# Weights of the second output projection moved into the spent tiles of keys and queries, and split during the attention

## Chip, cores, metric

The kernel runs on one core of a Trainium2 chip. The metric is device microseconds of one execution, median over runs; lower is better.

## What is computed

Two layers of a diffusion backbone on 512 latent and 256 context tokens of width 1024, all in 32-bit floats. What matters here, of each layer:

```python
y  = concatenate([y_fn, y_na, y_gla]) @ w_out      # Fourier mixing, neighbourhood attention (6 heads x 64), linear attention
x  = x + g_m * y
x  = x + g_f * swiglu(ada_modulate(x, norm_ffn, sh_f, sc_f), ffn_w1, ffn_w3, ffn_w2)
if need_ctx:                                       # first layer only
    yc = concatenate([fourier_mix(fc), ctx_attn(qch, kch, vch), yc_gla]) @ w_out
    cx = cx + cg_m * yc
    cx = cx + cg_f * swiglu(ada_modulate(cx, ...), ffn_w1, ffn_w3, ffn_w2)
```

## The kernel before

**Arithmetic.** Every 32-bit operand of a product is split into a high part (a copy on ACT, L195) and a low part (source minus high part, on DVE, L189; on POOL where the caller says so). `split` at L197 does both, and a product is then three matmuls (`mm3`, L181). Tiles are feature-major: 128 features by 512 latent columns (or two halves of 256) or 256 context columns.

**The second output projection.** `w_out` is applied in two pieces. The first (`woa`, 5 blocks of 128 rows, generator `wo`) covers Fourier mixing and linear attention; its products are dropped between the units of the attention by `fill`. The second (`wob`, 3 blocks of 128 rows, generator `wb`) covers the neighbourhood attention and runs behind it. `wout` (L969) makes both. For each of 8 output tiles m it has a raw weight (128 x 384, 192 KB), its split, and one product with each stream n, each ending in a residual update on DVE (L192, `u<-m,u,u` and the like). In layer 0 the streams are context (256 columns) and latents (512 columns); in layer 1 only latents, in two halves.

**Buffers of `wb` before.** In layer 0 (`whole` false) two raw tiles and two split tiles `whl` rotate; raw tile m + 2 is loaded when weight m + 1 is split, in the loop over products. `split_at` = 6 gives context and latent tile in turn for m = 0 to 5, then context tiles 6 and 7, then latent tiles 6 and 7. In layer 1 (`whole` true) all eight weights are split into eight tiles `whlw` during the attention, out of the two raw tiles in turn.

**The attention.** It has 3 pairs of heads with 5 blocks each in layer 0 (15 units), 4 in layer 1 (12 units). Unit n on PE: scores of unit n (`a<-st,st`), transposes of unit n - 1 (`b<-u,p`, L1244), some products of `wo` (`m<-u,whl`), then values of unit n - 1 (`y<-pT,vn`). DVE adds the bias and takes the maximum (`s<-a,bias`, L1212), ACT takes the exponential (`p<-s,nm`), DVE scales it (`p<-p,rcl`, L1223), and the transposed tile `pT` is copied out of PSUM by ACT or DVE in turn. `kn` and `qn` (6 tiles of 128 x 512 each, pool `nap`) hold normalised keys and queries; pairs 1 and 2 are transposed out of them by `features_of_heads` (L942) during the units of the pair before, and stored by 8 DMAs `st<-kt` and then `st<-qt` on SP (L909). After the last of these `kn` and `qn` are read no more, though they stay allocated to the end of the attention.

**What stands behind `wb`.** The sum of squares of each updated tile (`nsq` on ACT; added up on DVE for context, as `nacc` on POOL for latents in layer 0), the norm factors (`nms`, `nrs`, `ndg`), the modulation of eight context and eight latent tiles (`nt<-u,u,a` DVE, `u<-nt,u` ACT, `u<-nt,u,u` DVE), and the first two steps of the FFN. Those use four weights of 128 x 1024 (`W_first`, L1368, two steps of two), loaded by DMA `raw<-in_w` into three raw tiles (L430); ACT makes the high parts, POOL the low parts.

**What sets the order.** PE's order in the attention and in `wb` is the order of the code (`tc.manual_schedule`, L1291 and L1328). Elsewhere a scheduler at build time orders each engine's instructions by its own model of time and by priorities; `W_first` has the priority of the start of `wb` (`early_w`, L1336). At run time each engine, and SP with its DMAs, goes through its list in order.

Of the kernel before, what the change touches and what calls it, by code (L numbers as in the profile page):

```python
# [16 lines left out]
F32 = mybir.dt.float32  # L17
F32R = mybir.dt.float32r
# [7 lines left out]
KD = 8  # L26
# [116 lines left out]
def hybrid_kernel(tc, d, out, dbg=None):  # L143
    nc = tc.nc
# [283 lines left out]
    def wraw(p, src, n, rb, cap):  # L428
        r = mk(p, [128, cap], F32, "raw", rb)[:, :n]
        nc.sync.dma_start(out=r, in_=src)  # L430
        return r
# [23 lines left out]
    for l in range(DEPTH):  # L455
# [508 lines left out]

        gm = lambda s, k: modT[l][:, s, 16 + k:17 + k]

        loaded = []

        def wout(src, nk, streams, kinds, whole=False, split_at=KD, begin=0):  # L969

            nb, cap = (KD, 128 * nk) if whole else (2, 640)
            tag = "whl" + "w" * whole
            raw = lambda m: wraw(wop, src[m], 128 * nk, 2, cap)
            part = lambda r: wsplit(wop, r, (nk, 128), nb, cap, tag)
            if whole:
                w = [part(raw(m)) for m in range(KD)]  # L980
            else:
                raws = [raw(m) for m in range(2)]
                w = [part(raws[0])]
            early = {}
            for m in range(0, begin, 2):
                yield None, 0
                bank = (PM, PB, PM)[m // 2]()
                for i in range(2):
                    ps = bank[:, 256 * i:256 * i + 256]
                    for j in range(nk - 1):  # L990
                        mm3(ps, w[m + i][0][:, j], w[m + i][1][:, j], streams[0][0][j][:, 0], streams[0][0][j][:, 1],
                            i == j == 0, False)
                    early[m + i, 0] = ps, nk - 1
            yield None, 0

            def product(m, n, ys, xs, s):
                wh, wl = w[m]
                ps, j0 = early.pop((m, n), (None, 0))
                ps = dense(kinds)[:, :xs(m).shape[-1]] if ps is None else ps
                for j in range(j0, nk):  # L1000
                    mm3(ps, wh[:, j], wl[:, j], ys[j][:, 0], ys[j][:, 1], j == 0, j == nk - 1)
                    if j < nk - 1:
                        yield None, ps.shape[-1]
                stt(xs(m), ps, gm(s, m), xs(m), ALU.mult, ALU.add)

            todo = [(m, n) for m in range(split_at) for n in range(len(streams))]
            todo += [(m, n) for n in range(len(streams)) for m in range(split_at, KD)]
            if begin:
                todo[:2 * begin:2], todo[1:2 * begin:2] = todo[:begin], todo[begin:2 * begin]
            for m, n in todo:  # L1010
                if m == KD - 1:
                    loaded.append(src)
                if m + 1 == len(w) < KD:
                    w.append(part(raws[m + 1]))
                    if m + 2 < KD:
                        raws.append(raw(m + 2))
                yield from product(m, n, *streams[n])
                yield (m, n), streams[n][1](m).shape[-1]

# [134 lines left out]

        nst = ExitStack()
        np_ = pool(nst, f"na{l}", "left")

        credit = [0.0]

# [123 lines left out]

        half = lambda ts, h: [t[..., 256 * h:256 * h + 256] for t in ts]
        streams = both_x(ync, ynl) if ctx_q else [(half(ynl, h), lambda m, h=h: xl[m][:, 256 * h:256 * h + 256], 0) for h in range(2)]
        wb = wout(d["wob"][l], 3, streams, "mbmya", not ctx_q, 6 if ctx_q else 0, 0 if ctx_q else 4)

        nb = 5 if ctx_q else 4
        units = [(pr, b) for pr in range(3) for b in range(nb)]
# [1 line left out]
        with tc.manual_schedule(engines={mybir.EngineType.PE}):  # L1291
            for n in range(len(units) + 1):
                if n < len(units):
                    pr, b = units[n]
                    pairs[pr].scores(b)
                if n:
                    pq, c = units[n - 1]
                    pairs[pq].transposed(c)
                if n == len(units) and not ctx_q:
                    for _ in wo:  # L1300
                        pass
                if loaded and not ahead:
                    ahead.append(next(wb))
                if n == len(units) and not ctx_q:
                    next(wb)
                if n < len(units) and b == 0 and pr < 2:
                    pairs[pr + 1] = Heads(pr + 1)
                fill(2.4 if ctx_q else 2.3)
                if pr < 2 and n < len(units):
                    for _ in range((1, 1, 1, 1, 0)[b]):  # L1310
                        next(pairs[pr + 1].prepare, None)
                if n == nb - 1:
                    with tc.issue_after(last_stack[0]):
                        load_streams(range(3, KD))
                if n:
                    pairs[pq].values(c)
            for _ in wo:
                pass
            if not ctx_q:
                for _ in range(1):  # L1320
                    next(wb)
# [164 lines left out]
```

## Time and profile before

| | |
|---|---|
| median of 3 runs | 1663.78 us (1663.53 to 1668.41) |
| the profiled execution | 1662.66 us |
| its span | 1660.6 us |
| PE busy | 97% |
| DVE, ACT, POOL busy | 55%, 35%, 14% |

The span runs from the first to the last instruction that the profiler saw; 2.06 us of the profiled execution lie outside. Layer 0's attention lies at 312 to 397 us of the span and its `wb` at 397 to 429; layer 1's attention lies at 1200 to 1275. A PE busy for 97% of the span means that a change can only remove the remaining gaps, the stretches at half clock, or work. In a list of one engine's rows, the bracket at a row's end is how long the engine was idle before it and what ended that.

### The profile page before, as it was taken

To read this page: it belongs to the slowest core of one execution; us is meant where nothing else is said; L and a number is where in the kernel's file an instruction comes from. 1 tells how busy PE (TensorE), PEld (TensorE's weight loads), DVE (VectorE), ACT (ScalarE), POOL (GpSimd) and SP (SyncE) were. 2 spreads that over 40 slices of the span, in tenths; PEclk is the share of its full clock that TensorE was granted. 3 is DMA by queue.
4 is the path that set the end of the run, shared out by engine and by line. 5 is a ranking of instruction groups with operands and counts; after the bars stand their busy time and mean duration, and the time that the engine had idled before them with its cause. 6 is when DMAs were issued, how large, how long until landed. Compare 5 with 4: busy or idle time off the path is not lost.

```text
span 1660.6 us, 25071 instructions
## 1 busy us (share of the span) xinstructions
PE 1613.8 (97%) x9938; PEld 1402.3 (84%) x9938; DVE 920.6 (55%) x1665; ACT 583.9 (35%) x1048; POOL 232.2 (14%) x275
## 2 busy tenths in 40 slices
PE   6999999999999999999999999999999999999999
PEld 5878889787888888888888889899787988888887
DVE  5699974776774664355333434464577743434432
ACT  5365223544542411211122324842445522222220
POOL 0143431003240400000000011333102000000000
PEclk9999999999999999999999999999999999999999
DMA  9445544653152454144221411222663233233321
GB/s 329 159 151 164 164 155 124 192 134 112 52 175 76 153 188 143 62 148 146 65 75 45 127 53 40 70 97 94 194 182 119 84 113 99 91 93 98 102 89 51
DMA packets 79904, 199.66 MB, mean 120 GB/s; under 512 B 10344, under 2 KB 21164, under 8 KB 78764
## 3 DMA queue, kind: packets, MB, share of 16 engines
q1 hardware_dynamic: 79788, 198.07, 37.9%
q8 instruction: 78, 1.28, 0.3%
q14 instruction: 38, 0.31, 0.1%
HBM read 174.84 MB, written 14.29 MB: 114 GB/s over the span
## 4 chain that ended last, share of the span: by engine, by line
PE 81%; DVE 7%; DMA 6%; ACT 2%; issue 2%; SPq 1%; POOL 0%; DVEq 0%; ACTq 0%; POOLq 0%
PE a L181 26%; PE m L181 23%; PE b L181 19%; PE y L181 11%; DVE adac L192 2%; DMA adaw<-in_adaw 2%; DVE u L192 1%; DVE whl L189 1%; PE b L1244 1%; DMA raw<-in_wg 1%; DMA raw<-in_wob 1%; DMA raw<-in_w 1%; ACT whl L195 1%; DMA qn<-scr_q 1%; DVE u L189 1%
## 5 line engine op out<-in xcount | busy, mean ns | idle before, releaser
L195 ACT ACTIVATE whl<-raw 128x1024 fp32r<-128x1024 f32 (+7 forms) x222 | 205.0, 928 | 392.2 <-PE a L181 132.3
L189 DVE TENSOR_TENSOR whl<-raw,whl 128x1024 fp32r<-128x1024 f32 (+7 forms) x201 | 225.2, 1122 | 91.7 <-ACT whl L195 91.5
L181 PE MATMUL m<-u,whl 128*128 128x512 f32 (+1 forms) x1278 | 264.1, 359 | 1.9 <-DVE whl L189 1.9
L181 PE MATMUL a<-u,whl 128*128 128x512 f32 (+1 forms) x1299 | 246.6, 346 | 2.4 <-ACT u L195 1.5
L181 PEld LDWEIGHTS m<-u,whl 128*128 128x128 f32 x1278 | 211.9, 191 | 35.3 <-DVE whl L189 2.2
L181 PEld LDWEIGHTS a<-u,whl 128*128 128x128 f32 x1299 | 208.6, 189 | 32.6 <-ACT u L195 1.7
L181 PE MATMUL b<-u,whl 128*128 128x512 f32 (+1 forms) x915 | 181.8, 349 | 1.8 <-ACT whl L195 0.9
L192 DVE SCALAR_TENSOR_TENSOR adac<-adaw,u,adac 128x512 f32<-128x512 f32 x196 | 159.0, 828 | 42.1 <-DMA adaw<-in_adaw 41.0
L181 PEld LDWEIGHTS b<-u,whl 128*128 128x128 f32 x915 | 150.1, 189 | 25.2 <-ACT whl L195 1.1
L181 PE MATMUL b<-whl,u 128*128 128x384 f32 (+1 forms) x696 | 144.9, 345 | 1.3 <-DVE u L192 0.9
L181 PE MATMUL m<-whl,u 128*128 128x384 f32 (+2 forms) x672 | 138.0, 344 | 2.8 <-ACT u L195 2.5
L181 PEld LDWEIGHTS b<-whl,u 128*128 128x128 f32 x696 | 122.2, 189 | 8.7 <-issue 4.7
L181 PEld LDWEIGHTS m<-whl,u 128*128 128x128 f32 x672 | 116.5, 189 | 15.3 <-issue 9.8
L181 PE MATMUL a<-g,whl 128*128 128x512 f32 (+1 forms) x594 | 126.9, 370 | 0.7 <-DVE g L189 0.7
L181 PEld LDWEIGHTS a<-g,whl 128*128 128x128 f32 x594 | 103.9, 189 | 19.8 <-DVE g L189 1.2
L181 PE MATMUL y<-u,whl 128*128 128x512 f32 (+1 forms) x420 | 83.6, 353 | 1.0 <-DVE u L189 1.0
L192 DVE SCALAR_TENSOR_TENSOR ft<-ft,a 128x512 f32<-128x512 f32 (+1 forms) x53 | 30.5, 576 | 95.0 <-ACT ft L195 63.0
L181 PEld LDWEIGHTS y<-u,whl 128*128 128x128 f32 x420 | 69.2, 192 | 12.7 <-DVE u L189 1.4
L181 PE MATMUL m<-g,whl 128*128 128x512 f32 (+1 forms) x396 | 77.8, 350 | 0.0
L181 PEld LDWEIGHTS m<-g,whl 128*128 128x128 f32 x396 | 64.8, 189 | 9.7
L181 PE MATMUL b<-g,whl 128*128 128x256 f32 (+1 forms) x396 | 72.4, 336 | 0.0
L189 POOL TENSOR_TENSOR nacc<-nacc,nsq 128x512 f32<-128x512 f32 (+1 forms) x14 | 15.0, 1074 | 400.2 <-ACT nsq L195 400.2
(220 smaller groups left out, 1983.6 us busy)
## 6 DMA issues: line engine op xcount, KB each, us to landing
raw<-in_w SPq DMA_DIRECT2D x104, 512.0 KB, 3.9
adaw<-in_adaw SPq DMA_DIRECT2D x48, 512.0 KB, 3.8
adaw<-in_adaw SPq DMA_DIRECT2D x64, 256.0 KB, 3.0
raw<-in_wg SPq DMA_DIRECT2D x40, 384.0 KB, 3.4
raw<-in_w SPq DMA_DIRECT2D x32, 448.0 KB, 3.4
adaw<-in_ada SPq DMA_DIRECT2D x8, 1024.0 KB, 10.5
st<-kt SPq DMA_DIRECT2D x32, 192.0 KB, 4.1
raw<-in_woa SPq DMA_DIRECT2D x16, 320.0 KB, 8.8
```

Of the source, the lines that this page charges most:

```text
L181: last_mm[0] = T.matmul(o, lhsT=l, rhs=r, start=start, stop=stop, skip_group_check=True).ins
L189: e.tensor_tensor(out=o, in0=a, in1=b, op=op)
L192: V.scalar_tensor_tensor(out=o, in0=a, scalar=s, in1=b, op0=op0, op1=op1)
L195: S.activation(out=o, in_=i, func=f, **kw)
L1244: T.transpose(ps[:, 128 * j:128 * j + 128], p[:, 128 * j:128 * j + 128], ident)
```

## The change

Four edits in `wout` and its callers:

1. `place(n)` names the tiles `kn0` to `kn5` and `qn0` to `qn5` again. Layer 0: raw weights of `wb` go alternately to `kn0` and `kn1`; the splits of weights 0 to 4 go to (`kn2`, `kn3`), (`kn4`, `kn5`), (`qn0`, `qn1`), (`qn2`, `qn3`), (`qn4`, `qn5`), all during the attention; weights 5 and 6 go to the two old `whl` tiles and weight 7 to (`kn2`, `kn3`) again. Layer 1: the eight raw weights go to `kn0` to `kn5`, `qn0`, `qn1`, loaded together behind the last store of `st`, and are split to `whlw` as before.
2. The first step of `wb` is taken at unit 2 * nb (10 of 15, 8 of 12) and no longer when `wo` reaches its last weight; in the loop a split is made up to two weights ahead.
3. `split_at` in layer 0 goes from 6 to 5: context tiles 5, 6, 7 come before latent tiles 5, 6, 7.
4. The tags `s`, `p`, `pT` of the attention's pool are allocated at its opening, which moves addresses only.

```diff
-        loaded = []
+        def place(n):
+            return mk(nap, [128, 512], F32, [f"kn{j}" for j in range(6)][n] if n < 6 else f"qn{n - 6}")

-        def wout(src, nk, streams, kinds, whole=False, split_at=KD, begin=0):
+        def wout(src, nk, streams, kinds, whole=False, split_at=KD, begin=0, places=None):
...
-            raw = lambda m: wraw(wop, src[m], 128 * nk, 2, cap)
-            part = lambda r: wsplit(wop, r, (nk, 128), nb, cap, tag)
+            def raw(m):
+                if places is None:
+                    return wraw(wop, src[m], 128 * nk, 2, cap)
+                r = place(m if whole else m % 2)[:, :128 * nk]
+                nc.sync.dma_start(out=r, in_=src[m])
+                return r
+            def part(r):
+                m = len(w)
+                if places is None or whole or m in (5, 6):
+                    return wsplit(wop, r, (nk, 128), nb, cap, tag)
+                hh, ll = [place(2 + 2 * (m % 5 if m < 5 else 0) + i)[:, :128 * nk].bitcast(F32R) for i in range(2)]
+                split(r, hh, ll)
+                return [a.rearrange("p (a b) -> p a b", a=nk) for a in (hh, ll)]
+            w = []
             if whole:
-                w = [part(raw(m)) for m in range(KD)]
+                with tc.issue_after(last_stack[0]):
+                    raws = [raw(m) for m in range(KD)]
+                for r in raws:
+                    w.append(part(r))
+            elif places:
+                raws = [raw(m) for m in range(2)]
+                for m in range(5):
+                    w.append(part(raws[m]))
+                    raws.append(raw(m + 2))
             else:
                 raws = [raw(m) for m in range(2)]
-                w = [part(raws[0])]
+                w.append(part(raws[0]))
...
-                if m == KD - 1:
-                    loaded.append(src)
-                if m + 1 == len(w) < KD:
-                    w.append(part(raws[m + 1]))
-                    if m + 2 < KD:
-                        raws.append(raw(m + 2))
+                if len(w) <= m + (2 if places else 1) and len(w) < KD:
+                    w.append(part(raws[len(w)]))
+                    if len(raws) < KD:
+                        raws.append(raw(len(raws)))
...
+        for tag, shape, bufs in (("s", [128, 512], 2), ("p", [128, 512], 4), ("pT", [128, 4, 128], 3)):
+            mk(np_, shape, F32, tag, bufs)
...
-        wb = wout(d["wob"][l], 3, streams, "mbmya", not ctx_q, 6 if ctx_q else 0, 0 if ctx_q else 4)
+        wb = wout(d["wob"][l], 3, streams, "mbmya", not ctx_q, 5 if ctx_q else 0, 0 if ctx_q else 4, True)
...
-                if loaded and not ahead:
+                if n == 2 * nb and not ahead:
                     ahead.append(next(wb))
```

The scheduler then gives other orders at the places below. (Line numbers of the changed kernel are some 10 to 25 higher than before from L970 on.)

POOL in layer 0, from the end of the attention to the start of the FFN, before. `whl` are the low parts of `W_first`, `nacc` the latents' squares, `nrs` the norm factors (128x2 context, 128x4 latents):

```order
L189 TENSOR_TENSOR whl_4955<-raw_4953,whl_4955 128x1024
L189 TENSOR_TENSOR whl_4960<-raw_4958,whl_4960 128x1024
L189 TENSOR_TENSOR whl_4965<-raw_4963,whl_4965 128x1024
L189 TENSOR_TENSOR whl_4970<-raw_4968,whl_4970 128x1024
L189 TENSOR_TENSOR nacc_4649<-nacc_4649,nsq_4712 128x512
L189 TENSOR_TENSOR nacc_4649<-nacc_4649,nsq_4745 128x512
L189 TENSOR_TENSOR nacc_4649<-nacc_4649,nsq_4778 128x512
L189 TENSOR_TENSOR nacc_4649<-nacc_4649,nsq_4811 128x512
L189 TENSOR_TENSOR nacc_4649<-nacc_4649,nsq_4844 128x512
L189 TENSOR_TENSOR nrs_4897<-nms_4895,u_63 128x2
L189 TENSOR_TENSOR nacc_4649<-nacc_4649,nsq_4889 128x512
```

The same place in the changed kernel:

```order
L189 TENSOR_TENSOR nacc_4679<-nacc_4679,nsq_4824 128x512
L189 TENSOR_TENSOR nrs_4892<-nms_4890,u_63 128x2
L189 TENSOR_TENSOR nacc_4679<-nacc_4679,nsq_4884 128x512
L189 TENSOR_TENSOR nacc_4679<-nacc_4679,nsq_4905 128x512
L189 TENSOR_TENSOR nacc_4679<-nacc_4679,nsq_4926 128x512
L189 TENSOR_TENSOR whl_4964<-raw_4962,whl_4964 128x1024
L189 TENSOR_TENSOR nrs_5076<-nms_5074,u_63 128x4
L189 TENSOR_TENSOR whl_4969<-raw_4967,whl_4969 128x1024
L189 TENSOR_TENSOR whl_4974<-raw_4972,whl_4974 128x1024
L189 TENSOR_TENSOR whl_4979<-raw_4977,whl_4979 128x1024
```

The four low parts stood ahead of all of POOL's sums, and now stand behind the last of them, one ahead of the latents' norm factors and three behind.

ACT in layer 0, at the modulation of the context tiles, in the changed kernel (`u<-nt,u` are the modulated tiles, `nsq_4926` the squares of the last latent tile, `whl` the high parts of `W_first`):

```order
L195 ACTIVATE nsq_4905<-u_3410 128x512
L195 ACTIVATE u_4954<-nt_4982,u_106 128x256
L195 ACTIVATE u_4955<-nt_4986,u_106 128x256
L195 ACTIVATE nsq_4926<-u_3408 128x512
L195 ACTIVATE u_4956<-nt_4990,u_106 128x256
L195 ACTIVATE u_4957<-nt_4994,u_106 128x256
L195 ACTIVATE whl_4964<-raw_4962 128x1024
L195 ACTIVATE u_4958<-nt_4998,u_106 128x256
L195 ACTIVATE whl_4969<-raw_4967 128x1024
L195 ACTIVATE u_4959<-nt_5002,u_106 128x256
L195 ACTIVATE whl_4974<-raw_4972 128x1024
L195 ACTIVATE u_4960<-nt_5006,u_106 128x256
```

Before, the four `whl` rows of `W_first` stood among the first dozen rows of ACT behind the attention; now the first stands behind the fourth modulated context tile, and the fourth some ten rows further on. On PE the first FFN steps of the context, before in turn over both halves of step 0 (`a`, `b`), now take all eight k of the first weight, then of the second, third and fourth.

DVE in layer 1, from the first split of `wob` on, before (`s` is the bias step of unit 8, `whlw` are low parts of `wob`; `p<-p,rcl` ends a head's softmax, and PE transposes `p` next):

```order
L189 TENSOR_TENSOR whlw_12475<-raw_12473,whlw_12475 128x384
L1212 ISA s_12305,mx_12304<-a_12298,bias_12024 128x512
L1212 ISA mx_12304 128x1
L1212 ISA s_12316,mx_12315<-a_12299,bias_12027 128x512
L1212 ISA mx_12315 128x1
L1250 COPY pT_12338<-b_12333 128x512
L192 SCALAR_TENSOR_TENSOR u_11663<-m_12210,u_107,u_11663 128x512
L1222 RECIPROCAL rcl_12312<-sml_12310 128x1
L189 TENSOR_TENSOR whlw_12480<-raw_12478,whlw_12480 128x384
L1223 TENSOR_SCALAR p_12309<-p_12309,rcl_12312 128x512
L1222 RECIPROCAL rcl_12323<-sml_12321 128x1
L1223 TENSOR_SCALAR p_12320<-p_12320,rcl_12323 128x512
```

The same place in the changed kernel, from the third split on (the first two stand ahead of the first `s` of unit 8, which stands ahead of this piece):

```order
L189 TENSOR_TENSOR whlw_12374<-kn_2209_12356,whlw_12374 128x384
L1237 ISA s_12328,mx_12327<-a_12311,bias_12039 128x512
L1237 ISA mx_12327 128x1
L189 TENSOR_TENSOR whlw_12377<-kn_2210_12358,whlw_12377 128x384
L189 TENSOR_TENSOR whlw_12380<-kn_2211_12360,whlw_12380 128x384
L1275 COPY pT_12350<-b_12345 128x512
L192 SCALAR_TENSOR_TENSOR u_11672<-m_12222,u_107,u_11672 128x512
L1247 RECIPROCAL rcl_12324<-sml_12322 128x1
L189 TENSOR_TENSOR whlw_12383<-kn_2212_12362,whlw_12383 128x384
L189 TENSOR_TENSOR whlw_12386<-qn_2213_12364,whlw_12386 128x384
L189 TENSOR_TENSOR whl_12396<-raw_12220,whl_12396 128x640
L1248 TENSOR_SCALAR p_12321<-p_12321,rcl_12324 128x512
```

Before, one split stood ahead of the bias steps of unit 8 and one ahead of its first `p`; now seven stand ahead of its first `p`, and the eighth, a low part of values and the next unit's two bias steps between its first and its second `p`. On ACT the first five high parts stand ahead of the copy `pT` of unit 7 and of both exponentials of unit 8. Behind these the order in layer 1 is the old one.

## Rows read from the trace of the kernel before

**Rows 1.** Stretches: length, busy PE, PEld, DVE, ACT, POOL; PEclk; DMA share, GB/s.

```profile
370.00:380.00 10.00, 10.00 (x72) 8.24 (x72) 8.38 (x22) 4.83 (x12) 0.83 (x4) 1.00 0.08 22
404.00:411.00 7.00, 5.14 (x22) 4.22 (x21) 5.53 (x7) 3.77 (x8) 7.00 (x4) 0.76 0.50 161
1199.90:1203.30 3.40, 2.67 (x9) 2.22 (x10) 2.69 (x7) 1.46 (x4) 0.43 (x2) 0.83 0.96 301
```

**Rows 2.** PE's timeline in layer 0's second projection: start, us, what.

```profile
397.51 1.33 PE L181 MATMUL y<-u,whl 128*128 128x256 f32 x9 [0.95 <-DVE u L189]
...
406.02 1.46 PE L181 MATMUL m<-u,whl 128*128 128x256 f32 x8 [1.86 <-DVE whl L189]
407.28 3.61 PE L181 MATMUL y<-u,whl 128*128 128x512 f32 x9
...
411.79 2.23 PE L181 MATMUL m<-u,whl 128*128 128x512 f32 x9
413.86 1.24 PE L181 MATMUL b<-u,whl 128*128 128x256 f32 x9
...
422.24 0.38 PE L181 MATMUL b<-u,whl 128*128 128x256 f32 x1 [0.87 <-ACT whl L195]
...
426.31 2.33 PE L181 MATMUL y<-u,whl 128*128 128x512 f32 x9
```

**Rows 3.** DVE's timeline there and at the modulation behind it.

```profile
403.55 2.42 DVE L189 TENSOR_TENSOR whl<-raw,whl 128x384 fp32r<-128x384 f32 x1 [1.04 <-ACT whl L195]
...
429.34 0.86 DVE L192 SCALAR_TENSOR_TENSOR nt<-u,u,a 128x256 f32<-128x256 f32 x2
430.58 1.66 DVE L192 SCALAR_TENSOR_TENSOR u<-nt,u,u 128x256 fp32r<-128x256 f32 x2 [0.38 <-ACT u L195]
...
433.21 0.48 DVE L192 SCALAR_TENSOR_TENSOR u<-nt,u,u 128x256 fp32r<-128x256 f32 x1 [0.18 <-ACT u L195]
```

**Rows 4.** POOL's timeline in the same stretch.

```profile
403.18 7.69 POOL L189 TENSOR_TENSOR whl<-raw,whl 128x1024 fp32r<-128x1024 f32 x3 [2.74 <-DMA raw<-in_w]
...
413.06 2.16 POOL L189 TENSOR_TENSOR nacc<-nacc,nsq 128x512 f32<-128x512 f32 x1 [0.94 <-ACT nsq L195]
416.79 1.29 POOL L189 TENSOR_TENSOR nacc<-nacc,nsq 128x512 f32<-128x512 f32 x1 [1.57 <-ACT nsq L195]
...
433.94 1.20 POOL L189 TENSOR_TENSOR nrs<-nms,u 128x4 f32<-128x4 f32 x1 [2.38 <-DVE nms L395]
```

**Rows 5.** ACT by line and form from 396 to 406 us: busy us, mean ns.

```profile
L195 ACT ACTIVATE whl<-raw 128x1024 fp32r<-128x1024 f32 x4 | 4.2, 1049 | 2.2 <-DMA raw<-in_w 2.2
```

**Rows 6.** PE's timeline at the start of layer 0's FFN.

```profile
442.38 3.16 PE L181 MATMUL b<-u,whl 128*128 128x256 f32 x25
445.38 0.86 PE L181 MATMUL m<-u,whl 128*128 128x512 f32 x3
```

**Rows 7.** PE's timeline in layer 1: attention's start, then units 8 and 9.

```profile
1200.63 1.19 PE L181 MATMUL a<-st,st 128*128 128x512 f32 x4 [2.83 <-DVE st L192]
...
1249.30 1.20 PE L181 MATMUL a<-st,st 128*128 128x512 f32 x4 [1.56 <-DMA raw<-in_wob]
...
1256.13 1.04 PE L1244 MATMUL b<-u,p 128*128 128x128 f32 x8
...
1259.52 1.33 PE L181 MATMUL y<-pT,vn 128*64 128x128 f32 x16 [0.29 <-DVE u L189]
```

**Rows 8.** DVE's timeline in the same units; unit 8's second softmax ends with 1255.14.

```profile
1250.59 0.56 DVE L189 TENSOR_TENSOR whlw<-raw,whlw 128x384 fp32r<-128x384 f32 x1 [3.64 <-ACT whlw L195]
1251.07 0.68 DVE L1212 CUSTOM_DVE_ANT_0 s<-a,bias 128x512 f32<-128x512 f32 x1
...
1255.14 0.49 DVE L1223 TENSOR_SCALAR p<-p,rcl 128x512 f32<-128x512 f32 x1
1255.54 0.82 DVE L189 TENSOR_TENSOR whl<-raw,whl 128x640 fp32r<-128x640 f32 x1
```

**Rows 9.** SP's timeline in layer 0: the issue of one DMA.

```profile
386.78 0.33 SPq L430 DMA_DIRECT2D raw<-in_wob  x1
```

## Prediction

> **What bounds the kernel now.** The table of the profiled execution comes first: PE is busy for 97% of the span, so only its gaps, its half-clock stretches and its work count. The change takes no work off PE; it moves weights and their splits. So I read the two places that it touches on PE's timeline, layer 0's second projection and layer 1's attention from unit 8 on, and then DVE, POOL and ACT at the same times.
>
> In layer 0 the projection runs from 397.51 to 428.64 us, 31.1 us [rows 2]. A latent tile that waits for nothing takes 2.07 us (411.79 to 413.86), a context tile 1.08 (1.24 less the 0.16 by which such rows overlap). Eight of each, and 0.6 for the sums between them and the last tile's full length, make 25.8 us. So 5.3 us are lost. The reader sees where: 1.86 us of waiting for a low part of a weight, then a latent tile of 3.61 us in place of 2.23, then 0.87 us for a high part. The long tile is the clock: 404 to 411 us has a mean granted clock of 0.76 [rows 1], which is 3.4 us at 1.2 GHz instead of 2.4 within seven.
>
> The wait of 1.86 us has a plain origin: DVE's split of a 128x384 weight took 2.42 us [rows 3] while POOL was in the three low parts of the FFN's first weights, 7.69 us from 403.18 on [rows 4]. The same form takes 0.56 us on DVE elsewhere [rows 8].
>
> **The change part by part, layer 0's projection.** Weights 0 to 6 are split before it begins, or nearly, and POOL's low parts are gone from it. The wait of 1.86, its half clock and the 0.87 go: 5.3 us less, and the last latent product ends near 397.5 + 25.8 = 423.3 and not at 428.64. The 0.95 us ahead of the first product [rows 2] stays, since it waits for the last values.
>
> **The splits in the attention.** Five splits move into units 9 to 12: 0.56 us each on DVE, 2.8 together, and about as much on ACT. PE is busy for 10.00 of 10 us there, DVE for 8.38 [rows 1]. The bound below is nothing (PE has no gap there to win, so no gain either), above 2.8 us if DVE had no room. DVE's 1.6 free us in ten cover most: I take 0.5. SP's DMAs of `wob` move ahead of `st<-qt`, at 0.33 us an issue [rows 9]; these stores are due units later, so I cost them at nothing, and at 0.33 each if that cover were gone.
>
> **The start of the FFN in layer 0.** This is where I expect most of the gain to go back. The four high parts of `W_first` now stand on ACT among the context's modulations, and POOL's four low parts behind its last sum, so they begin after the projection instead of under it. From the end of the last product: 1.6 us for the residual update and a pair of `nt` (428.64 to 430.20 before [rows 2, 3]), two modulated low parts of 0.48 to 0.83 [rows 3], some 0.5 for ACT's modulated tiles: 3.5 us, 426.8. ACT's high part 1.05 [rows 5]: 427.85. POOL's first low part at 7.69 / 3 = 2.56: 430.4. The norm factors of the latents, 1.20 [rows 4]: 431.6. Three more low parts: 439.3. Then 23 matmuls on the last weight at 3.16 / 25 each [rows 6]: 442.2. Before, this phase ended at 445.38 [rows 6], paced by the modulations. So of 5.3 us 3.2 remain. PE however idles for some seven us ahead of 430.4, and a wait of 1.86 was enough for 3.4 us at half clock. With that PE itself is the bound: 96 matmuls, 12.1 us, and 1.7, from 430.4 on: 444.2, a gain of 1.2. I take a gain of 2.0, between the two. The ends: 4.9 if POOL is never late (first high part 0.4 earlier, low parts overlapping the norm factors), and a loss of 3.7 if DVE and POOL hold each other up in every low part (below).
>
> Those two engines do disturb each other: two `u<-nt,u,u` took 1.66 us instead of two times 0.48 while POOL added squares [rows 3], and an addition on POOL took 2.16 instead of 1.29 [rows 4]. The Trainium skill (SBUF — State Buffer, "Who interferes with whom") says that a DVE instruction with two inputs in SBUF and a POOL instruction that reads SBUF exclude each other, whichever began first holding the port for its whole length. The rows agree (2.42 for 0.56, 2.16 for 1.29). By that rule each of POOL's four low parts waits for at most one DVE low part of 0.48, the phase ends at 444.1, and the gain is 1.3 where the sum without it has 3.2; my 2.0 lies between these too.
>
> **Layer 1's attention.** Here eight weights are loaded at once, and their splits crowd ahead of the softmax of unit 8. DVE starts on the first split at 1250.59 as before, when the DMA has come; PE's wait ahead of the scores, 1.56 us [rows 7], stays, as the scores read the stores `st` that were issued earlier. The profile puts that wait down to a load of `wob`, which no score reads. Before, the second `p` of unit 8 ended at 1255.14 + 0.49 = 1255.63 [rows 8]. Ahead of it DVE now also does six splits at 0.48 from start to start (1250.59 to 1251.07), the 128x640 low part of 0.82, the next unit's two bias steps of 0.68 and a low part of values of about half a microsecond: 2.9 + 0.8 + 1.3 + 0.5 = 5.5, less half a microsecond of idle time that it fills: 1260.6. PE's four transposes of that head began at about 1256.65 (half of the 1.04 us from 1256.13 [rows 7]) and now wait until 1260.65, in three waits (values of unit 7, each head): 4.0 us. In return later small waits, three of about the 0.29 us at 1259.52 [rows 7], go, as the splits are done: 0.8. I take +3.2. The ends: a gain of 0.8 if the splits cost nothing, and 4.0 + 1.7 = 5.7 with a stretch at half clock on top. The three waits lie under 2.5 us each, and 1.56 alone left the clock whole, while 2.83 us of idle time up to 1200.63 [rows 7] were followed by a mean of 0.83 [rows 1].
>
> **Sum.** -2.0 + 0.5 + 3.2 = +1.7 us. Fewer stalls of `wb` are paid for at two other places. Against the profiled execution of 1662.66 us that is 1664.4; the median of the runs is 1.1 higher, 1663.78, and gives **1665.5**. About 0.3%, or 5 us, is what a measurement of this kernel can tell from no change.
>
> **The rivals.**
>
> *Faster.* The loss in layer 0 is as small as can be (-4.9) and layer 1's splits hide (-0.8), the attention's too: -5.7, 1658.1. For it: POOL's list is not long, and PE's fill work in the attention usually covers DVE. Against: an engine's list is gone through in order, and the splits stand ahead of `p`. Chance 0.14.
>
> *Slower.* POOL's low parts at the FFN's start take as long against DVE's modulations as the addition did, 2.16 / 1.29 = 1.67 times: 10.25 us become 17.1, the last low part comes at 446.2, the phase ends at 449.1, 3.7 later than before. With 0.5 and 3.2: +7.4, 1671.2. It decides once the phase ends beyond 446.7 (then the sum is over 5), which is low parts of 3.7 us each and not 2.56. For it: the two engines alternate on just such instructions. Against: three low parts in a row took only 7.69 us with DVE beside them [rows 4]. The rule above gives less than this too. Chance 0.20.
>
> *Nothing moves.* The FFN's weights give back all of the 5.3 us, and the fill work on PE hides layer 1's splits: 0 to +0.5, 1664. This is the case where the second projection was hidden anyway. Chance 0.08.
>
> **How the numbers follow.** My forecast has 0.58, and its own range is -2 to +5. Faster by over 0.3% comes from the first rival and a little of the forecast's low end: 0.15. Slower comes from the second and the upper end of the forecast, where half clock comes at both places: 0.22. The rest, 0.63, is within 0.3%. The range: from 1659.5, most of the way to the faster rival, to 1671.0, just short of the slower one.
>
> **What would show it.** In the changed profile: the projection of layer 0 in 26 us without the 1.86; POOL's four `whl` rows after the last `nacc`; PE idle for several microseconds ahead of the first FFN matmul on a `whl`; the first latent step of the FFN between 441 and 445 (span times; 445.38 before); in layer 1 a wait of PE for `p` of unit 8 with a second of more than 1 us, and DVE's eight `whlw` rows all before 1261. I am wrong if the latent FFN step comes before 440, if layer 1's attention ends no later than before relative to its start, or if `wb` still waits for a weight in layer 0.

## The result, and the profile after

The changed kernel is slower: 1673.73 us, median of 20 runs (1667.24 to 1676.94), against 1663.03 us, median of 20 runs (1660.11 to 1673.05), for the kernel before beside it. The ratio is 1.0051, 95% interval 1.0041 to 1.0062: some 8.5 us, 6.8 to 10.3; the two medians themselves lie 10.7 us apart. The forecast was 1665.5 us and no change that can be told, range 1659.5 to 1671.0.

The profiled execution of the changed kernel took 1667.65 us, with a span of 1665.8 us, 5.2 more than before's 1660.6. So this trace shows a little over half of the loss; where the rest is comes further down.

**Layer 0, the second projection and the FFN behind it.** PE's timeline after:

```profile
397.41 1.34 PE L181 MATMUL y<-u,kn 128*128 128x256 f32 x9 [0.95 <-DVE u L189]
...
421.40 2.30 PE L181 MATMUL y<-u,kn 128*128 128x512 f32 x9
427.61 0.38 PE L181 MATMUL a<-u,whl 128*128 128x256 f32 x1 [3.91 <-ACT whl L195]
...
430.05 4.00 PE L181 MATMUL a<-u,whl 128*128 128x256 f32 x17 [1.27 <-POOL whl L189]
...
436.65 0.51 PE L181 MATMUL a<-u,whl 128*128 128x256 f32 x2 [0.90 <-DVE u L192]
...
437.58 3.00 PE L181 MATMUL a<-u,whl 128*128 128x256 f32 x23
440.42 5.80 PE L181 MATMUL b<-u,whl 128*128 128x256 f32 x47
446.06 0.86 PE L181 MATMUL m<-u,whl 128*128 128x512 f32 x3
```

From the first product to the end of the last one: 397.41 to 423.70, 26.3 us where it was 31.1 [rows 2]. The waits of 1.86 and 0.87 us and the long tile are gone. But then PE waits 3.91 and 1.27 us for the FFN's first weight and 0.90 us for a modulated context tile, and the first latent product of the FFN starts at 446.06, against 445.38 [rows 6]. From first product to there it is 48.65 us, before 47.87: all that the projection gained is given back, and 0.8 more. What PE waits for stands on POOL, ACT and DVE (POOL's timeline, then ACT's, then DVE's):

```profile
427.64 2.36 POOL L189 TENSOR_TENSOR whl<-raw,whl 128x1024 fp32r<-128x1024 f32 x1 [1.01 <-ACT whl L195]
...
431.43 7.41 POOL L189 TENSOR_TENSOR whl<-raw,whl 128x1024 fp32r<-128x1024 f32 x3
```

```profile
426.52 1.04 ACT L195 ACTIVATE whl<-raw 128x1024 fp32r<-128x1024 f32 x1
```

```profile
428.27 2.00 DVE L192 SCALAR_TENSOR_TENSOR u<-nt,u,u 128x256 fp32r<-128x256 f32 x1 [0.18 <-ACT u L195]
...
431.62 4.97 DVE L192 SCALAR_TENSOR_TENSOR u<-nt,u,u 128x256 fp32r<-128x256 f32 x2
```

Before, POOL's four low parts ran at 398 to 411 us, three of them in [rows 4] and the first here:

```profile
398.03 2.41 POOL L189 TENSOR_TENSOR whl<-raw,whl 128x1024 fp32r<-128x1024 f32 x1 [14.55 <-ACT whl L195]
```

Now they run from 427.64 to 438.84, and ACT's high part of the first weight starts at 426.52. DVE's low parts of the modulated tiles take 2.00 us for one and 4.97 for two beside them, against 0.48 [rows 3]; POOL's own take 2.36 and 7.41 / 3 = 2.47, no more than before. And the clock falls to half, and is back at 436 us (stretches; the column after the engines is PEclk):

```profile
427.50:431.00 3.50, 2.12 (x13) 2.03 (x14) 3.32 (x6) 3.03 (x6) 2.93 (x2) 0.68 0.00 1
431.00:434.50 3.50, 3.50 (x19) 3.50 (x18) 3.46 (x4) 2.85 (x7) 3.50 (x3) 0.50 0.46 149
434.50:438.00 3.50, 2.60 (x17) 2.31 (x17) 2.23 (x2) 0.69 (x2) 3.50 (x2) 0.84 0.63 198
438.00:441.50 3.50, 3.50 (x31) 3.50 (x30) 3.50 (x5) 2.44 (x4) 0.84 (x1) 1.00 0.68 217
```

```profile
436.00:446.00 10.00, 9.35 (x78) 9.35 (x79) 8.73 (x15) 4.59 (x7) 2.84 (x2) 1.00 0.74 223
```

0.32 + 0.50 + 0.16 of 3.5 us each are 3.4 us, which is 6.9 us at 1.2 GHz. But it is not this half clock that sets 446.06. PE stood idle for 1.27 us of it, and it was over when PE stopped once more, for the 0.90 us. What PE waited for there is the last of DVE's low parts, done at 431.62 + 4.97 = 436.59. Of the 96 matmuls of the context's first steps 72 stood behind this wait (2 + 23 + 47), and PE needed 9.4 us for them at full clock, from 436.65 to 446.06. PE goes through its list in order, so a faster PE before would have come to the same wait earlier and stood there longer. The two other traces with these late weights show the same: 1.15 and 1.02 us of waiting for DVE behind the half clock, then 9.4 us. So by the traces the loss at the start of the FFN is DVE held up beside POOL; no run kept the weights late and took POOL out of DVE's way.

**Layer 0, attention unit 10.** A wait that before did not have. PE's, ACT's and SP's timelines:

```profile
355.26 0.38 PE L955 MATMUL b<-u,qn 128*128 128x128 f32 x2
...
363.25 1.21 PE L181 MATMUL a<-st,st 128*128 128x512 f32 x4 [1.31 <-DMA st<-qt]
```

```profile
353.94 0.53 ACT L195 ACTIVATE qn<-kn 128x384 fp32r<-128x384 f32 x1 [3.71 <-DMA kn<-in_wob]
...
356.26 0.51 ACT L195 ACTIVATE qn<-kn 128x384 fp32r<-128x384 f32 x1
356.67 0.46 ACT L195 ACTIVATE qt<-b,qg 128x256 fp32r<-128x256 f32 x1
```

```profile
357.15 2.39 SPq L909 DMA_DIRECT2D st<-qt  x4
```

PE had transposed these queries by 355.64, but ACT took them at 356.67 only. Two splits of weights of `wob` stood ahead of them in its list: at the first ACT stood idle for 3.71 us until the weight's DMA had landed, and a copy and two exponentials came behind it; the second came right ahead of the queries. Before, ACT had been waiting for them, and PE's scores of unit 10 waited for nothing (ACT's row, then PE's):

```profile
357.34 0.47 ACT L195 ACTIVATE qt<-b,qg 128x256 fp32r<-128x256 f32 x1 [1.40 <-PE b L955]
```

```profile
363.37 1.19 PE L181 MATMUL a<-st,st 128*128 128x512 f32 x4
```

So the stores of the queries left a microsecond late, and PE waited 1.31 us for them.

**Layer 1, units 8 and 9.** PE's timeline, and DVE's at the two softmax ends:

```profile
1251.49 1.25 PE L181 MATMUL a<-st,st 128*128 128x512 f32 x4 [1.39 <-DMA kn<-in_wob]
...
1257.17 1.09 PE L181 MATMUL y<-pT,vn 128*64 128x128 f32 x14 [0.44 <-DVE pT L1275]
...
1260.04 0.63 PE L1269 MATMUL b<-u,p 128*128 128x128 f32 x4 [0.64 <-DVE rcl L1247]
1262.65 0.63 PE L1269 MATMUL b<-u,p 128*128 128x128 f32 x4 [1.98 <-DVE p L1248]
```

```profile
1252.81 1.08 DVE L189 TENSOR_TENSOR whlw<-kn,whlw 128x384 fp32r<-128x384 f32 x2 [3.50 <-ACT whlw L195]
...
1259.42 0.47 DVE L1248 TENSOR_SCALAR p<-p,rcl 128x512 f32<-128x512 f32 x1
...
1262.03 0.47 DVE L1248 TENSOR_SCALAR p<-p,rcl 128x512 f32<-128x512 f32 x1
```

Three new waits, 0.44 + 0.64 + 1.98 = 3.1 us, in the three forecast places: the second head's `p` ends 9.7 us after DVE's first split, before 5.0 [rows 8]. Of the small waits behind, that of 0.29 us [rows 7] is gone. The three differences, +0.8, +1.3 and +2.8 (worked out below), make 4.9 of the 5.2 us. Two more partly cancel, and the rest are smaller ones: PE was 1.7 us earlier than before when it began on the queries of unit 10 (355.26 against 356.92), and it lost 1.1 us at a wait in layer 1's linear attention (last section).

### The profile page after: what moved, and what is told of

It is laid out like the page before. It is cut to its first block, busy times and chain, and to the rows that moved or that the text cites. A ratio compares the mean times of both kernels' runs of the same rounds, so it can differ in the third digit from the quotient of the medians.

```text
span 1665.8 us, 25067 instructions
## 1 busy us (share of the span) xinstructions
PE 1612.0 (97%) x9938; PEld 1401.9 (84%) x9938; DVE 923.4 (55%) x1665; ACT 584.6 (35%) x1048; POOL 232.2 (14%) x275
## 5 line engine op out<-in xcount | busy, mean ns | idle before, releaser
L195 ACT ACTIVATE whl<-raw 128x1024 fp32r<-128x1024 f32 (+6 forms) x214 | 201.1, 943 | 389.5 <-PE a L181 131.3
L189 DVE TENSOR_TENSOR whl<-raw,whl 128x1024 fp32r<-128x1024 f32 (+6 forms) x193 | 217.3, 1127 | 92.4 <-ACT whl L195 91.4
L181 PE MATMUL m<-u,whl 128*128 128x512 f32 (+1 forms) x1233 | 255.2, 359 | 0.0
L181 PE MATMUL a<-u,whl 128*128 128x512 f32 (+1 forms) x1281 | 242.8, 347 | 6.1 <-ACT whl L195 3.9
L181 PEld LDWEIGHTS m<-u,whl 128*128 128x128 f32 x1233 | 204.8, 191 | 32.4 <-issue 0.8
L181 PE MATMUL b<-u,whl 128*128 128x512 f32 (+1 forms) x897 | 177.3, 350 | 0.7 <-DVE u L192 0.7
L181 PE MATMUL y<-u,whl 128*128 128x512 f32 (+1 forms) x393 | 76.3, 348 | 0.0
L181 PEld LDWEIGHTS y<-u,whl 128*128 128x128 f32 x393 | 63.7, 189 | 10.4 <-issue 0.8
```

What stands on the lines that cost most here:

```text
L181: last_mm[0] = T.matmul(o, lhsT=l, rhs=r, start=start, stop=stop, skip_group_check=True).ins
L189: e.tensor_tensor(out=o, in0=a, in1=b, op=op)
L195: S.activation(out=o, in_=i, func=f, **kw)
```

## The experiments

Times are medians of 9 to 12 runs, beside 23 to 35 runs of the kernel before on the same chip. The last column, the stretch, is the time from the first product of layer 0's projection to the FFN's first latent product in the kernel's trace.

| kernel | median, us | before, us | ratio, 95% interval | stretch, us |
|---|---|---|---|---|
| the change, again | 1672.89 | 1664.50 | 1.0038, 1.0019 to 1.0057 | 48.63 |
| layer 0 alone | 1668.51 | 1664.50 | 1.0023, 1.0006 to 1.0040 | 48.65 |
| layer 1 alone | 1670.22 | 1664.50 | 1.0029, 1.0011 to 1.0047 | 46.33 |
| layer 0 alone, own pool | 1658.90 | 1664.50 | 0.9970, 0.9953 to 0.9988 | 40.97 |
| layer 1 alone, spread | 1664.11 | 1664.28 | 0.9994, 0.9981 to 1.0007 | 46.21 |
| layer 0 alone, own pool, late splits | 1658.44 | 1664.28 | 0.9967, 0.9951 to 0.9982 | 40.97 |
| all three repairs | 1657.72 | 1664.28 | 0.9965, 0.9950 to 0.9981 | 40.99 |
| the three tags alone | 1664.56 | 1664.28 | 1.0008, 0.9993 to 1.0022 | 45.99 |
| the change, own pool | 1666.77 | 1664.73 | 1.0003, 0.9990 to 1.0016 | 40.99 |
| all three repairs, split_at 6 | 1659.56 | 1664.73 | 0.9970, 0.9956 to 0.9983 | 42.63 |

In the three kernels with the old code in layer 0 (layer 1 alone, with and without spread splits, and the tags alone) the last column has 46.0 to 46.3 us, and not the 47.87 of the trace of before. They have the wait for DVE in the projection too, but no half clock behind it, as here with the tags alone, where the latent tile behind the wait takes 2.23 us and not 3.61 [rows 2]:

```profile
405.72 1.23 PE L181 MATMUL m<-u,whl 128*128 128x256 f32 x8 [1.99 <-DVE whl L189]
406.79 2.23 PE L181 MATMUL y<-u,whl 128*128 128x512 f32 x9
```

So the half clock there belongs to one of four traces, and against the other three the change loses 2.3 to 2.7 us at this place, not 0.8.

The theory after the first trace: three losses that have nothing to do with each other (late weights at the FFN, late queries ahead of unit 10, a late softmax in layer 1), each with its part of half clock. The rival: one of them carries it all, and the others cost nothing in the runs. Edits are shown against the changed kernel, with "..." where lines are left out.

**The change again** (no edit).

> The changed kernel once more, unaltered, for a second trace and for the granted clock of each run. Its profiled execution was only 5.2 us longer in span than before's, while the median of the runs is some 9 to 10 us longer; so about half of the loss lies in executions that the first trace does not show. If half-clock stretches make the difference, time falls by about 1.7 us for each 0.001 that the mean granted clock is higher, and the runs at 0.991 have two or three stretches more than the runs at 0.995. If instead waits differ from run to run, the time varies at one clock.

From run to run of one kernel it is largely the clock: the fastest of the first 20 runs of the change, at a mean granted clock of 0.995, took 1667.24 us, the slowest, at 0.989, 1676.94, and 0.006 of 1670 are 10.0 us for a difference of 9.7. Between the kernels it is the smaller part. Over these 12 runs of the change the mean clock is 0.9928 and over the 35 runs of before beside them 0.9940: 2 us of 1670. At one and the same clock, 0.992, five runs of the change have a mean of 1673.7 us and six of before 1667.7, 6 us less.

The span of this execution is 1674.5 us, 8.7 more than in the first trace of the same kernel, and it shows where stretches at half clock come and go. One lies behind a wait in layer 1's linear attention (PE's row, then the stretch):

```profile
1088.48 1.65 PE L181 MATMUL a<-u,u 128*128 128x192 f32 x4 [2.25 <-DVE u L192]
```

```profile
1086.00:1093.00 7.00, 4.75 (x30) 4.56 (x23) 3.41 (x8) 4.73 (x8) 0.13 (x1) 0.76 0.45 139
```

The first trace has the same wait, of 2.25 us, and a clock of 1.00 behind it. The other lies at layer 1's first scores:

```profile
1200.00:1208.00 8.00, 5.30 (x24) 4.19 (x24) 2.71 (x6) 2.05 (x6) 0.00 (x0) 0.77 0.68 181
1208.00:1216.00 8.00, 5.58 (x18) 4.26 (x17) 5.60 (x13) 3.26 (x8) 0.44 (x2) 0.59 0.93 229
```

Three waits of PE stand there (0.85 and 1.52 us for `qn<-scr_q`, 2.42 for `st`), where the first trace has one, of 2.83, and 0.79 and 1.00 in the two stretches. The two places make 1.7 and 3.4 of the 8.7 us by the clock. The second is not the change's own: the kernel with all three repairs has 0.57 from 1188 to 1200 us. Waits inside the change's own places were as in the first trace (3.91 at the FFN, 1.19 at unit 10, 0.67 and 1.98 in layer 1).

**Layer 0 alone and layer 1 alone.** The places, the tags and the new start of the loads in one layer, the old code in the other (here layer 0 alone; for layer 1 alone it is 6 in place of 5, and `(0, 1)`):

```diff
-        for tag, shape, bufs in (("s", [128, 512], 2), ("p", [128, 512], 4), ("pT", [128, 4, 128], 3)):
+        for tag, shape, bufs in (("s", [128, 512], 2), ("p", [128, 512], 4), ("pT", [128, 4, 128], 3)) if (1, 0)[l] else ():
...
-        wb = wout(d["wob"][l], 3, streams, "mbmya", not ctx_q, 5 if ctx_q else 0, 0 if ctx_q else 4, True)
+        wb = wout(d["wob"][l], 3, streams, "mbmya", not ctx_q, 5 if ctx_q else 0, 0 if ctx_q else 4, (1, 0)[l] or None)
...
-                if n == 2 * nb and not ahead:
+                if (n == 2 * nb if (1, 0)[l] else loaded) and not ahead:
```

> Only layer 0 has the change (weights in the spent tiles, early trigger, three latent tiles last); layer 1 is as before. If the late weights at the start of layer 0's FFN are what costs (PE idle 3.9 and 1.3 us, then half clock), this is slower than before by 1 us as in the first trace, up to 5 us. If layer 1's softmax is the cause, it equals before within 1 us, or is a little faster.

> Only layer 1 has the change (eight weights loaded together and split ahead of the softmax of unit 8); layer 0 is as before. If the crowd of splits is what costs, slower than before by 3 us (waits of PE of 0.4, 0.6 and 2.0 us in the first trace), up to 6 us with half clock behind them. If layer 0 is the cause, equal to before within 1 us.

Both lose: 4.0 us by the medians (1.0 to 6.7 by the interval) and 5.7 (1.8 to 7.8). Their sum, 9.7 by the medians and 8.7 by the ratios, agrees with the whole loss of 6.8 to 10.3, and neither interval reaches down to no loss; so it is not one layer alone, and that much of the rival is out. The two places of layer 0 are not told apart by this. With layer 1 alone PE's waits in layer 1 are the same as with the whole change:

```profile
1257.88 0.63 PE L1276 MATMUL b<-u,p 128*128 128x128 f32 x4 [0.67 <-DVE rcl L1254]
1260.50 0.63 PE L1276 MATMUL b<-u,p 128*128 128x128 f32 x4 [1.99 <-DVE p L1255]
```

**A pool of their own for keys, queries and values.** The theory: the FFN's weight pool is built where the pool `nap` lies, and with the change the last reader of a tile of `nap` is the projection's last product. The edit takes keys, queries and values, and with them the reused tiles, out of `nap`. (This one in layer 0 alone, as above.)

```diff
+        nkp = pool(yst, f"nk{l}", "right")
         nap = pool(yst, f"nq{l}", "right")
...
-            tiles_of_heads(nap, nm, dst)
+            tiles_of_heads(nkp, nm, dst)
...
-            return mk(nap, [128, 512], F32, [f"kn{j}" for j in range(6)][n] if n < 6 else f"qn{n - 6}")
+            return mk(nkp, [128, 512], F32, [f"kn{j}" for j in range(6)][n] if n < 6 else f"qn{n - 6}")
```

> As the run with layer 0 alone, but keys, queries and values lie in a pool of their own, so that the pool under the FFN's weights is free when the attention ends. By the build's order POOL's four low parts then stand ahead of its sums again, as before the change. If the release of that pool is what made the FFN's weights late, PE's wait ahead of the FFN goes back to under 2 us and the kernel is faster than before by 2 to 5 us (the waits of the second projection are gone, unless DVE's few remaining splits there meet POOL's low parts). If the weights are late for another reason, it is like the run with layer 0 alone.

It is faster than before, by 5.6 us at the medians. The stretch of 48.65 us falls to 40.97, and the build puts POOL's four low parts ahead of its sums again. So it was the pool of the reused tiles that held the FFN's weights back: the splits, the loads and their places are those of layer 0 alone. The same in the kernel with all three repairs (PE, then POOL):

```profile
423.86 0.62 PE L181 MATMUL a<-u,whl 128*128 128x256 f32 x3 [0.77 <-DVE u L192]
...
437.30 0.86 PE L181 MATMUL m<-u,whl 128*128 128x512 f32 x3
```

```profile
396.83 2.41 POOL L189 TENSOR_TENSOR whl<-raw,whl 128x1024 fp32r<-128x1024 f32 x1 [14.54 <-ACT whl L195]
399.65 7.47 POOL L189 TENSOR_TENSOR whl<-raw,whl 128x1024 fp32r<-128x1024 f32 x3 [0.41 <-ACT whl L195]
```

POOL is at the low parts while PE does the projection. One split of `wob` is still left to DVE there and takes 2.05 us in place of 0.55, but PE does not wait for it. DVE's modulations come later, away from POOL's low parts (0.9 to 1.1 us for two, with the pool in layer 0 alone), and PE's one wait ahead of the FFN is 0.77 us.

**Layer 1's splits two by two.** Behind the softmax of units 8 to 11, by issue order on ACT and DVE:

```diff
                 for r in raws:
-                    w.append(part(r))
+                    with tc.issue_after(last_p[0]), tc.issue_after(last_p[1]):
+                        w.append(part(r))
+                    if len(w) in (2, 4, 6):
+                        yield None, 0
...
+                if not ctx_q and 2 * nb < n < 2 * nb + 1 + 3:
+                    next(wb)
```

`last_p` holds the last exponential (ACT) and the last scaling of `p` (DVE) that were issued.

> As the run with layer 1 alone (eight weights loaded together into the spent tiles), but the splits stand two by two behind the softmax of units 8, 9, 10 and 11. If their place ahead of unit 8's softmax is what cost 3 us of waits there, those waits (0.7 and 2.0 us) go, and the time is that of before or up to 1 us less. If the loading of all eight at once is to blame (DMAs in the way of the stores), the waits stay and it is slower than before by 3 to 6 us.

The waits are gone, and the time is before's (-0.2 us; the interval reaches from -3.2 to +1.2). So the load of all eight weights at once costs nothing that can be told; the place of their splits on ACT and DVE did. PE's timeline at the same units:

```profile
1247.60 1.32 PE L181 MATMUL a<-st,st 128*128 128x512 f32 x4 [1.62 <-DMA st<-qt]
...
1252.48 1.09 PE L181 MATMUL y<-pT,vn 128*64 128x128 f32 x16
1253.50 1.20 PE L181 MATMUL a<-st,st 128*128 128x512 f32 x4
1254.54 1.04 PE L1279 MATMUL b<-u,p 128*128 128x128 f32 x8
1255.34 2.30 PE L181 MATMUL m<-u,whl 128*128 128x512 f32 x9
1257.57 1.09 PE L181 MATMUL y<-pT,vn 128*64 128x128 f32 x16
```

This trace names the stores `st<-qt` as what ends the wait of 1.62 us, which stays; before's named a load that no score reads [rows 7].

**Late splits in layer 0.** With the own pool, the five splits of the attention stand behind the softmax of unit 10:

```diff
                 for m in range(5):
-                    w.append(part(raws[m]))
+                    with tc.issue_after(last_p[0]), tc.issue_after(last_p[1]):
+                        w.append(part(raws[m]))
```

> As the run with layer 0 alone and a pool of its own, and the five splits in the attention stand behind the softmax of unit 10, so that none is ahead of the queries' high and low parts of the last pair. PE's wait of 1.2 us for the stores of the queries ahead of unit 10, which every trace with the change in layer 0 has and none without, should go; if the splits ahead of the queries on ACT cause it, 1 us faster than the run with its own pool alone. If it is the traffic of the weights' DMAs, the wait stays.

The wait ahead of unit 10 is gone. The edit moves two things: the splits on ACT, and with them loads of weights on SP, as a raw tile is loaded again only when its split is done (six loads now stand behind the stores, from 370.41 us on). ACT's delay is seen in the rows above; whether the loads beside the stores added to it is not told apart. In this trace (PE's rows, then ACT's):

```profile
363.56 1.09 PE L181 MATMUL y<-pT,vn 128*64 128x128 f32 x16
364.58 1.20 PE L181 MATMUL a<-st,st 128*128 128x512 f32 x4
```

```profile
358.55 0.47 ACT L195 ACTIVATE qt<-b,qg 128x256 fp32r<-128x256 f32 x1 [1.40 <-PE b L956]
```

In time the gain of a microsecond cannot be told from none: 0.9967 against 0.9970.

**All three repairs.**

> Both layers changed: own pool and late splits in layer 0, spread splits in layer 1. If the three repairs are independent, it is as fast as the best of the layer 0 runs, 6 to 7 us faster than before, and 14 us faster than the change. If layer 1's spread splits still cost, 3 us less than that.

0.9965: 6.6 us less than before at the medians and about 14 less than the change. The layer 1 edit adds nothing measurable to the layer 0 ones (1658.44 to 1657.72 us). Its median is the lowest of the study, but not told from the two above.

**The tags alone.** The fourth edit, in the kernel before.

> The kernel before with the fourth edit alone: the tags s, p and pT allocated at the opening of the attention's pool. All theories: equal to before within 1 us, since the order on every engine is the old one and only addresses differ.

1.0008, interval 0.9993 to 1.0022: nothing that can be told.

**The whole change with the pool alone repaired.**

> The whole change, with keys, queries and values in a pool of their own and nothing else repaired. If the late weights of the FFN are the largest of three separate losses, 8 us (48.65 to 40.97 us between the first product of the projection and the FFN's first latent product) come off the change's 8 to 10, and it lands within 2 us of before: the other two (1.2 us ahead of unit 10, 2.8 in layer 1) still stand against a gain of 6.9. If the losses hang together, it is further off, slower than before by over 3 us or as fast as all three repairs.

1.0003, interval 0.9990 to 1.0016: the pool takes the change from 8.5 us slower to no difference that can be told, as the sum of separate losses has it. The two other waits stand in its trace (1.22 us ahead of unit 10; 0.66 and 1.98 in layer 1), here with half clock behind the latter:

```profile
1262.00:1270.00 8.00, 6.33 (x35) 5.03 (x36) 4.42 (x14) 2.39 (x6) 0.52 (x2) 0.79 0.00 1
```

**The third edit.** All repairs with `split_at` 6 in layer 0.

> All three repairs, but the old order of the last tiles: context and latent tile 5 in turn, then the last two of each (split_at 6, not 5). The order of the last three latent tiles decides how early the context's sums are complete: with 6, one latent product of 2.07 us less lies behind the last context tile, so PE's wait ahead of the FFN (0.8 us with all repairs) should grow by up to 2 us. If the edit does nothing, the same time within 1 us.

The FFN's wait is 1.52 us in place of 0.77, and the stretch 42.63 us in place of 40.99:

```profile
426.69 0.51 PE L181 MATMUL a<-u,whl 128*128 128x256 f32 x2 [1.52 <-ACT u L195]
...
441.49 0.86 PE L181 MATMUL m<-u,whl 128*128 128x512 f32 x3
```

So three latent tiles last are worth 1.6 us in the trace: the context's sums are complete one product earlier, with more work of PE behind them. The runs, 1659.56 and 1657.72 us beside different runs of before, agree but do not prove it.

## Why the prediction was wrong

**The projection itself: right, but from one execution.** The waits of 1.86 and 0.87 us and the slow tile went. The last product ended at 423.70; forecast 423.3. But the 5.3 us to be won were those of one trace: the half clock in them is in none of the three other traces with the old code in layer 0.

**The start of layer 0's FFN: mis-sized, and the step that failed most.** I had -2.0 us for projection and FFN start together; the trace has +0.8 (48.65 against 47.87 us), and +2.3 to +2.7 against the three other traces of the old code. ACT and POOL did what the chain said: ACT's first high part at 426.52 (forecast 426.8), POOL's first low part done at 430.00 (430.4), its last at 438.84 (439.3). What failed is "With that PE itself is the bound: 96 matmuls, 12.1 us, and 1.7, from 430.4 on: 444.2", out of which I took the 2.0. PE could not do the 96 in one go. It stood at 435.75 with 72 of them left, until DVE's last modulated low part was done at 436.59, and those took it to 446.06 at full clock. I had DVE's low parts at 0.48 to 0.83 us; beside POOL's they took 2.00 for one and 4.97 for two. The half clock was twice as long as I had it, 6.9 us, but it lay ahead of this wait, so by the trace its length did not count. My own sign, a first latent step between 441 and 445, failed with it.

**Why the weights were late: not asked.** I read the new place of POOL's low parts from the order and costed it, which was right, but took it as given. It hung on the pool that the reused tiles belong to, and one more pool turns the edit into a gain.

**The splits in the attention: mis-sized.** I had 0.5 us, and wrote of the stores `st<-qt` that "these stores are due units later, so I cost them at nothing". They are due at unit 10, which begins 7.6 us after PE has transposed the queries in the trace of the change, and two splits ahead of them on ACT, the first with its wait for the weight, took 1 us of that. All five traces with layer 0's splits in the change's place have this wait, 1.2 to 1.3 us; the three with late splits don't.

**Layer 1: right.** +3.2 forecast, +2.8 in the trace (1251.49 to the next common wait at 1295.44 us is 43.95; before, 1249.30 to 1290.47, 41.17). The three waits came where they were named, and the repair by place alone shows the cause.

**The sum.** By the trace -2.0 + 0.5 + 3.2 should have read +0.8 + 1.3 + 2.8 = +4.9, and the one execution that the trace shows, 1667.65 us, lies inside the range. The median does not. In part that is because I took one profiled execution of before for all of them. Against the three other traces of the old code the first term is +2.3 to +2.7. With 1.3, 2.8 and the 1.1 in the linear attention, which was not in the sum, that makes 7.5 to 7.9 us from single traces, where the runs have 6.8 to 10.3. The lower mean clock of the runs is some 2 us of the loss; how much of that lies in the same places is open.

**The rivals.** *Slower* was the way it went, by another mechanism: POOL's low parts did not slow down at all; DVE's did, 2.00 for 0.48 and 4.97 for two. The rule of the Trainium skill (SBUF — State Buffer, "Who interferes with whom") says that whichever of the two engines issues first holds the shared pair of ports for its whole instruction, and the trace agrees: the DVE low part that began at 428.27, 0.6 us behind one of POOL's, ended at 430.27, 0.3 behind the end of POOL's, which took 2.36 as ever. I had priced its rule as a delay of POOL alone. *Faster* was forecast at 1658.1 us if layer 0's weights came in time and layer 1 cost nothing; the kernel with all three repairs, which is that case made, took 1657.72. That the numbers agree is partly luck: the rival had 4.9 us from layer 0 and 0.8 from layer 1, and the traces have 6.9 in layer 0 (47.87 to 40.99), or 5.0 to 5.3 against the three other traces, while layer 1 alone with spread splits gained nothing that can be told. *Nothing moves* is the change with its pool repaired, by accident: a gain in layer 0 and the losses elsewhere cancel.

## What to carry to other kernels

A tile that is reused past its stage keeps its whole pool alive; look at what is built over that pool, not only at the tile's address. Work that is moved under a busy engine must be placed behind what that engine's waiters need next: the same splits cost 3 us ahead of a softmax and nothing that could be told behind it. Where two engines hold each other up, price the delay on both sides, and ask which of them the critical one waits for last. And a stretch at half clock in a trace is that of one execution: before it is counted as a loss to be won back, look whether other traces of the same code have it.

## What was not expected of the hardware

A wait of PE in layer 1's linear attention, before which a weight (`raw<-in_wg`) lands, is 1.1 to 1.2 us in the four traces without a change in layer 0, 2.25 in the five with it and splits in the change's place, and 1.4 to 1.6 in the three with late splits. ACT stands idle ahead of it until that weight has landed, 2.61 us in the trace of before and 4.00 in that of the change. What delays the weight was not tried; the waits differ by 1.1 us, of the 4 that layer 0 alone loses, and cost more where half clock follows, as it does in three of the five.

One and the same wait is followed by half clock in one execution and not in another: that of 2.25 us by a stretch of 7 us at 0.76 in the second trace of the change and at 1.00 in the first, that of 1.98 us by 8 us at 0.79 with the pool repaired and at 1.00 in the first trace of the change.

The half clock at layer 1's first scores, which lie outside the places of the change, differs most. Over 1185 to 1220 us the mean granted clock is 0.95, 0.95, 0.95 and 0.90 in the four traces without a change in layer 0, and from 0.95 down to 0.80 in the eight with one. No run asks why.
